# A second line for the attention heads, and stick-breaking heads that ask for their values last

## The chip, the core and the metric

One Trainium2 chip, one core. The metric is device time in microseconds (us) of one execution of the kernel. A core has a matrix engine (TensorE, written PE in the profile, with its weight loads as PEld), a vector engine (VectorE, DVE), a scalar engine (ScalarE, ACT), GpSimd (POOL) and a queue of loads and stores (SyncE, SP). In the built program each engine has its own list of instructions; an instruction that waits holds up those that stand behind it in that list.

## What is computed

One layer of a hybrid encoder over 256 tokens of width 2048, in float32:

```python
h = rms_norm(x)                                   # x: (256, 2048)
proj = h @ w_in                                   # q, k, v of 8 "fox" heads, gates, q, k, v of 8 "sb" heads
# fox head: softmax(q_t.k_s/sqrt(128) + c[t] - c[s]), s <= t, times v; q and k are normed per head
# sb head:  z = q_t.k_s/sqrt(128); weights exp(log_sigmoid(z) + sum of log(1 - sigmoid) between s and t), s < t, times v
x = x + concat(rms_norm(out_fox), rms_norm(out_sb)) @ w_out
x = x + conv_ffn(rms_norm(x))                     # up-projection, width-3 causal convolution, SiLU gate, down-projection
```

## The kernel before

**Precision.** TensorE gets every float32 operand as a pair: `hi`, the value rounded to a shorter format (a copy on ScalarE, line 201), and `lo = raw - hi` (a subtraction on VectorE, line 202). A product is then three products: hi by hi, lo by hi, hi by lo.

**Steps.** All projections are cut into steps of 1 MB of weights. A step loads `w_raw` (line 194, three buffers in this part), makes `w_hi` and `w_lo` (two buffers each), and runs 16 matmuls on `w_hi` and then 8 (or 16 half-wide ones) on `w_lo`, all 512 columns or less: `token_major` (line 223; weights stream past the tokens) for values, fox queries and keys and `w_out`, `feature_major` (lines 250 and 257) for the stick-breaking queries and keys. Load and splits are written with a high priority, so they run about two steps ahead of their matmuls.

**What lies between the steps.** The attention itself is written as Python generators, each cut into stages by `yield`. They stand in one queue, `waiting`. After every step of a projection, `step()` (line 181) advances the first two generators of the queue (`WINDOW = 2`) by one stage each. So the order in which instructions are issued to the framework is: one step's matmuls, one stage each of two generators, the next step, and so on. The framework's scheduler then orders each engine's instructions by priority and by when it thinks their inputs are there. From the feed-forward part on, the order is written by hand and the scheduler changes nothing.

**The generators.**

- `fox_rows` (line 306): evicts a projection, norms q or k per head (square, sum, reciprocal root, product; lines 317 to 322), waits, transposes each 128-token tile on TensorE (line 298) and stores it in parts (lines 302, 304).
- `gates`: the forget gates and their running sum.
- `fox_head` (line 591): waits until the generators that stood in the queue when it was made are gone (`first`). Stage 1: scores (lines 598, 513), bias, mask and softmax (lines 605 to 619). After two more turns, stage 2: three transposes of the probabilities (line 624) and their split (627 to 629). Stage 3: the product with the values (581, 582) and `attended` (347 to 356), which stores the head's output and adds up its squares.
- `sb_head` (line 701). Stage 1: scores `ps_z` (lines 513, 708), the soft-plus on ScalarE (712 to 714), then `sp` (718, 719) and its split `sps` (721, 722). Stage 2: two products of `sps` with a triangular matrix, hi then lo, which make the suffix sums inside `ps_z` (727, 728), one exponential (730) and the split of the weights (732 to 736). Stage 3: as for a fox head. The tile `sp` has one buffer, `sps` and the score tiles (PSUM) have two, and so has the PSUM pool that holds transposes and head outputs.
- `next_rows`: transposes of the new x for the feed-forward part.

**The order of the projections:** in an opening written by hand the fox queries of heads 0 to 3, then fox values (with the gates' columns), fox keys of heads 0 to 3, fox queries and keys of heads 4 to 7, then for each half of the stick-breaking heads its queries, keys and values, then `w_out` in two groups of eight heads. A fox head joins the queue when its keys' generator has joined. A stick-breaking head joins once its half's values stand: it takes the tile `v` as an argument.

Of the kernel before, what the change touches and what calls it, by code (L numbers as in the profile page):

```python
# [36 lines left out]
WINDOW = 2  # L37
# [8 lines left out]
def hybrid_layer(  # L46
# [129 lines left out]
        return R  # L176


    waiting = deque()

    def step():
        for g in list(waiting)[:WINDOW]:
            if next(g, g) is g:
                waiting.remove(g)

    def finish():
        while waiting:
            step()


# [87 lines left out]
    with ExitStack() as actx:  # L278
# [9 lines left out]
        def project(c0, cols):  # L288
            return token_major(lambda k: hT[:, k], wi, 0, KT, c0, cols)
# [46 lines left out]
        def attended(po, h, g, group):  # L336

            if len(done) == NH:

                two = late.tile([P, 2, 2, S], F32R, name="oT89", tag="two_heads")  # L340
                oT.extend([two[:, 0], two[:, 1]])
                oT.extend(late.tile([P, 2, S], F32R, name=f"oT{i}") for i in range(NH + 2, 2 * NH - 4))
                oT.extend(hT[:, KT - 4 + i] for i in range(4))
            done.append(group * NH + h)
            assert done[-1] == len(done) - 1
            o = oT[group * NH + h]
            act.activation(o[:, 0, :], po, AF.Identity, scale=g[:, h : h + 1])
            dve.scalar_tensor_tensor(
                o[:, 1, :], po, g[:, h : h + 1], f32(o[:, 0, :]), op0=ALU.mult, op1=ALU.subtract
            )  # L350
            if h == 0:
                act.activation(ssq[group], po, AF.Square)
            else:
                sq = tmp.tile([P, S], F32, name="osq", tag="t1", bufs=3)
                act.activation(sq, po, AF.Square)
                dve.tensor_tensor(ssq[group], ssq[group], sq, op=ALU.add)
# [218 lines left out]
        def weighted(v, hs, w):  # L575


            wp, w1 = w
            po = psb.tile([P, S], F32, name="ps_o", tag="t")
            for i, (j, k) in enumerate(((0, 0), (0, 1), (1, 0))):  # L580
                nc.tensor.matmul(po, v[j][:, hs], wp[:, k], start=i == 0, stop=False)
            nc.tensor.matmul(po[:, P:], v[2][:, hs], w1, start=False, stop=True)
            return po
# [7 lines left out]
        def fox_head(h, qT, kT, first):  # L591
            while any(g in waiting for g in first):
                yield
            yield
            ps = pss.tile([P, 3, P], F32, name="ps_s", tag="s")
            s0, s1 = ps[:, 0, :], ps[:, 1:3, :].rearrange("p a b -> p (a b)")
            j = h % 4
            nc.tensor.matmul(s0, qT[0][0][:, j, :], kT[0][0][:, j, :], start=True, stop=False)
            of_parts(s1, [t[:, j, :] for t in qT[1][1:]], [t[:, j, :] for t in kT[2]], False, True)
            scored.append(h)  # L600
            pr = tmp.tile([P, 3, P], F32, name="pr", tag="pr")
            p0, p1 = pr[:, 0, :], pr[:, 1:3, :].rearrange("p a b -> p (a b)")

            for o, s, t in ((p0, s0, 0), (p1, s1, 1)):
                dve.scalar_tensor_tensor(
                    o, minus_c[h // 4][:, h % 4, : (t + 1) * P], c_of[:, t, h : h + 1], s, op0=ALU.add, op1=ALU.add
                )
            diagonal = pr[:, 0::2, :]
            dve.tensor_tensor(diagonal, diagonal, mask2, op=ALU.add)
            nm = small.tile([P, NT], F32, name="nm", tag="nm")  # L610
            dve.tensor_reduce(nm[:, 0:1], p0, axis=AX.X, op=ALU.max, negate=True)
            dve.tensor_reduce(nm[:, 1:2], p1, axis=AX.X, op=ALU.max, negate=True)
            l = small.tile([P, NT], F32, name="l", tag="l")
            act.activation(p0, p0, AF.Exp, bias=nm[:, 0:1], accum_out=l[:, 0:1])
            act.activation(p1, p1, AF.Exp, bias=nm[:, 1:2], accum_out=l[:, 1:2])
            rl = small.tile([P, NT], F32, name="rl", tag="rl")
            dve.reciprocal(rl, l)
            dve.tensor_scalar(p0, p0, rl[:, 0:1], None, op0=ALU.mult)
            dve.tensor_scalar(p1, p1, rl[:, 1:2], None, op0=ALU.mult)
            yield  # L620
            yield
            pt = pss.tile([P, 3, P], F32, name="ps_p", tag="s")
            for i in range(3):
                nc.tensor.transpose(pt[:, i, :], pr[:, i, :], ident)
            pT, pT1 = weights_tiles("pT")
            pt0 = pt[:, 0:2, :].rearrange("p a b -> p (a b)")
            act.copy(pT[:, 0], pt0)
            act.copy(pT1, pt[:, 2, :])
            dve.tensor_tensor(pT[:, 1], pt0, f32(pT[:, 0]), op=ALU.subtract)
            yield  # L630
            attended(weighted(vA, slice(h * HD, (h + 1) * HD), (pT, pT1)), h, g_fox, 0)

        for half in range(2):
            if half:
                qT = fox_queries(1)
                waiting.append(fox_rows(project(512, 512), qT, gq))
                step()
            else:
                qT = qT0
            kT = fox_keys(half)  # L640
            waiting.append(fox_rows(project(WF + 512 * half, 512), kT, g_k))
            step()
            first = list(waiting)
            for h in range(4 * half, 4 * half + 4):
                waiting.append(fox_head(h, qT, kT, first))


        B0 = 3 * WF + NH
# [52 lines left out]
        def sb_head(h, qT, kT, v):  # L701
            (q1, *q), (k1, *k) = qT[h % 4], kT[h % 4]
            ps = pss.tile([P, 3, P], F32, name="ps_z", tag="s")
            z0, z1 = ps[:, 0:2, :].rearrange("p a b -> p (a b)"), ps[:, 2, :]
            zz = ps.rearrange("p a b -> p (a b)")
            mm = nc.tensor.matmul
            of_parts(z0, k, q, True, False)
            mm(z1, k1, q1, start=False, stop=True)
            scored.append(NH + h)

            e = tmp.tile([P, 3 * P], F32, name="e", tag="pr")
            act.activation(e, zz, AF.Abs)
            act.activation(e, e, AF.Exp, scale=-1.0)
            act.activation(e, e, AF.Ln, bias=1.0)
            sp = tmp.tile([P, 3, P], F32, name="sp", tag="sp", bufs=1)
            diagonal = sp[:, 0::2, :]
            sp = sp.rearrange("p a b -> p (a b)")
            dve.scalar_tensor_tensor(sp, zz, 0.0, e, op0=ALU.max, op1=ALU.add)
            dve.tensor_tensor(diagonal, diagonal, limit2, op=ALU.min)
            sps = tmp.tile([P, 2, 3 * P], F32R, name="sps", tag="sps")  # L720
            act.copy(sps[:, 0, :], sp)
            dve.tensor_tensor(sps[:, 1, :], sp, f32(sps[:, 0, :]), op=ALU.subtract)
            yield

            for i in range(2):
                s = sps[:, i, :]
                mm(zz, ntri[:, :P], s, start=False, stop=False, skip_group_check=True)
                mm(ps[:, 1, :], ntri[:, P:], s[:, 2 * P :], start=False, stop=i == 1, skip_group_check=True)
            e = tmp.tile([P, 3, P], F32, name="e", tag="pr")
            act.activation(e, ps, AF.Exp)  # L730
            w, w1 = weights_tiles("w")
            dve.tensor_tensor(e[:, 0, :], e[:, 0, :], limit, op=ALU.min)
            e0 = e[:, 0:2, :].rearrange("p a b -> p (a b)")
            act.copy(w[:, 0], e0)
            dve.tensor_tensor(w1, e[:, 2, :], limit, op=ALU.min)
            dve.tensor_tensor(w[:, 1], e0, f32(w[:, 0]), op=ALU.subtract)
            yield
            attended(weighted(v, slice((h % 4) * HD, (h % 4 + 1) * HD), (w, w1)), h, g_sb, 1)

        for half in range(2):  # L740
            qT = sb_queries(half)
            kT = sb_keys(half)
            acc = project(B0 + 2 * WF + 512 * half, 512)

            assert scored[:4] == [0, 1, 2, 3]
            v = [
                at.tile([P, 512], dt, name=f"{name}{half}", tag=tag, bufs=1)
                for name, dt, tag in (("vB", F32R, "vB"), ("vBlo", F32R, "minus_c0"), ("vBt1", F32, "vBt1"))
            ]
            values(v, acc)  # L750
            for h in range(4 * half, 4 * half + 4):
                waiting.append(sb_head(h, qT, kT, v))


        ss2 = const.tile([P, NT, 4], F32, name="ss2")
# [398 lines left out]
```

## Time and profile before

| | |
|---|---|
| median of 3 runs | 1107.34 us (1106.92 to 1107.37) |
| span of the profiled execution (first to last instruction) | 1104.9 us |
| median less span (what lies around the span) | 2.4 us |
| TensorE busy in the span | 1099.6 us |
| VectorE, ScalarE, GpSimd busy | 870.4, 706.3, 44.0 us |
| attention part, from the first fox scores to the last head's product | about 123 to 345 us |

No device time of its own is listed for the profiled execution; its span stands 2.4 us below the median of the runs, and that distance is carried along unchanged in what follows.

Rows of groups read: line, engine, operation, output <- inputs, shapes, count | busy us, mean ns of one | idle time of the engine just before, and who ended it. Rows of a timeline read: start in us, length in us, engine, line, operation, names, shape, count, and in brackets the idle time before it. Matmuls overlap each other, so the length of a row of matmuls is longer than its share of TensorE's time: that share is the distance from its start to the start of the next row.

### The profile page before, as it was taken

The page shows a single profiled execution, that of the slowest core. Times are in us where ns is not written, and L with a number is a line of the kernel's source. Part 1 is how long each engine was busy: PE and PEld are TensorE (multiplying, and loading weights), DVE is VectorE, ACT ScalarE, POOL GpSimd, SP SyncE. Part 2 cuts the span into 40 slices and gives each one's busy share as a digit, 9 for nine tenths or more (in the row PEclk, how much of TensorE's full clock was granted, in tenths as well). Part 3 has the DMA queues.
Part 4 walks back from the last instruction along what each step waited for, and adds up shares of the span by engine and source line. Part 5 has one row for each costly group of instructions (what it writes and reads, how often), then busy time and mean ns, then how long its engine had stood idle before and what let it go on. Part 6 is the DMA issues. An engine that isn't in the chain of part 4 may idle for free. (4 is left out here: it accounts for less than half of the span.)

```text
span 1104.9 us, 14836 instructions
## 1 busy us (share of the span) xinstructions
PE 1099.6 (100%) x5880; PEld 953.9 (86%) x5880; DVE 870.4 (79%) x941; ACT 706.3 (64%) x879; POOL 44.0 (4%) x44
## 2 busy tenths in 40 slices
PE   9999999999999999999999999999999999999998
PEld 7998888888888888888888888888888888888887
DVE  6755767667676677679889888889798889889896
ACT  6543555457674567667767776667676677677753
POOL 0000000000000000000000010100000010100010
PEclk9999999999999999999999999999999999999999
DMA  8776555555644396557989597986979689987985
GB/s 285 195 232 229 187 164 180 173 170 169 242 156 158 114 304 200 190 189 195 301 210 323 191 229 264 260 269 178 315 210 306 213 218 281 245 264 196 324 212 168
DMA packets 179407, 246.09 MB, mean 223 GB/s; under 512 B 4432, under 2 KB 118890, under 8 KB 179082
## 3 DMA queue, kind: packets, MB, share of 16 engines
q1 hardware_dynamic: 162458, 209.87, 58.3%
q0 software_dynamic: 16560, 34.75, 16.7%
q8 instruction: 46, 0.75, 0.3%
q10 hardware_dynamic: 320, 0.53, 0.1%
q14 instruction: 23, 0.19, 0.0%
HBM read 243.02 MB, written 2.11 MB: 222 GB/s over the span
## 5 line engine op out<-in xcount | busy, mean ns | idle before, releaser
L202 DVE TENSOR_TENSOR w_lo<-w_raw,w_hi 128x2048 fp32r<-128x2048 f32 (+1 forms) x196 | 439.7, 2246 | 155.0 <-ACT w_hi L201 153.2
L201 ACT CAST w_hi<-w_raw 128x2048 fp32r<-128x2048 f32 (+1 forms) x196 | 367.1, 1875 | 247.4 <-PE pu L250 68.9
L250 PE MATMUL pu<-hT,w_hi 128*128 128x512 f32 x1664 | 396.7, 390 | 0.0
L250 PEld LDWEIGHTS pu<-hT,w_hi 128*128 128x128 f32 x1664 | 309.4, 188 | 62.6
L257 PEld LDWEIGHTS pu<-hT,w_lo 128*128 128x128 f32 x1664 | 213.7, 191 | 8.3
L257 PE MATMUL pu<-hT,w_lo 128*128 128x256 f32 x1664 | 216.4, 283 | 0.0
L223 PE MATMUL acc<-w_hi,hT 128*128 128x512 f32 (+1 forms) x576 | 124.9, 369 | 0.0
L223 PEld LDWEIGHTS acc<-w_hi,hT 128*128 128x128 f32 x576 | 101.2, 188 | 14.2
L201 ACT CAST w_hi<-w_sum 128x2048 fp32r<-128x2048 f32 x30 | 57.2, 1908 | 42.0 <-PE pu L250 35.8
L202 DVE TENSOR_TENSOR w_lo<-w_sum,w_hi 128x2048 fp32r<-128x2048 f32 x30 | 68.7, 2290 | 19.0 <-ACT w_hi L201 19.0
L851 ACT ACTIVATE tap<-up,ccol 128x256 f32<-128x256 f32 x176 | 74.6, 495 | 0.0
L223 PE MATMUL acc<-w_lo,hT 128*128 128x512 f32 (+1 forms) x288 | 64.6, 366 | 0.0
L223 PEld LDWEIGHTS acc<-w_lo,hT 128*128 128x128 f32 x288 | 51.6, 188 | 7.5
L956 POOL DMA_DIRECT2D w_sum<-in_w_down_dram x20 | 25.7, 1284 | 742.8 <-DVE w_lo L202 732.1
L223 PE MATMUL acc<-w_hi,oT 128*128 128x512 f32 x192 | 46.5, 394 | 0.0
L223 PEld LDWEIGHTS acc<-w_hi,oT 128*128 128x128 f32 x192 | 35.4, 188 | 7.2
L223 PE MATMUL bank_a<-w_hi,s 128*128 128x512 f32 x160 | 40.1, 392 | 0.2 <-DVE x L933 0.2
L223 PE MATMUL bank_a<-w_hi,g 128*128 128x512 f32 x160 | 40.0, 392 | 0.0
L223 PE MATMUL bank_b<-w_hi,s 128*128 128x512 f32 x160 | 40.0, 392 | 0.0
L223 PEld LDWEIGHTS bank_a<-w_hi,s 128*128 128x128 f32 x160 | 28.8, 189 | 5.8 <-issue 0.6
L223 PEld LDWEIGHTS bank_a<-w_hi,g 128*128 128x128 f32 x160 | 28.9, 189 | 5.3
L223 PEld LDWEIGHTS bank_b<-w_hi,s 128*128 128x128 f32 x160 | 28.9, 189 | 5.2
(215 smaller groups left out, 1077.5 us busy)
## 6 DMA issues: line engine op xcount, KB each, us to landing
w_raw<-in_w_up_dram SPq DMA_DIRECT2D x88, 1024.0 KB, 7.9
w_raw<-in_w_down_dram SPq DMA_DIRECT2D x44, 1024.0 KB, 6.6
w_raw<-in_w_in_dram SPq DMA_DIRECT2D x36, 1024.0 KB, 5.3
w_sum<-in_w_down_dram POOLq DMA_DIRECT2D x20, 1024.0 KB, 10.3
w_raw<-in_w_out_dram SPq DMA_DIRECT2D x16, 1024.0 KB, 5.1
w_raw<-in_w_down_dram POOLq DMA_DIRECT2D x10, 1024.0 KB, 14.7
w_raw<-in_w_in_dram SPq DMA_DIRECT2D x12, 688.0 KB, 4.3
w_raw<-in_w_in_dram SPq DMA_DIRECT2D x6, 512.0 KB, 7.1
```

The source lines that it names most:

```text
L201: act.copy(hi[:, :n], raw[:, :n])
L202: dve.tensor_tensor(lo[:, :n], raw[:, :n], f32(hi[:, :n]), op=ALU.subtract)
L223: nc.tensor.matmul(o, lhs(i, l, t), r[:, i, :], start=starts and j == 0, stop=stops and j == 3 * n - 1, skip_group_check=more,)
L250: nc.tensor.matmul(acc[:, j, :], hi[:, i, j * P : (j + 1) * P], hT[:, k].rearrange("p a b -> p (a b)"), start=k == 0, stop=False,)
L257: nc.tensor.matmul(acc[:, j, S:], lo[:, i, j * P : (j + 1) * P], hT[:, k, 0, :], start=False, stop=k == KT - 1,)
L851: act.activation(taps[w][:, j, :], u[:, j, w : w + S], AF.Copy, scale=ccol[:, w, f : f + 1])
L956: nc.gpsimd.dma_start(mem[into][:, : nk * 512].rearrange("p (a b) -> p a b", a=nk), src, accum_op=ALU.add)
```

## The change

There are two queues now: `waiting` for norms, gates and transposes, `heads` for all attention heads. `step()` advances the first two of each. A fox head's `first` then lists generators of `waiting` alone. A stick-breaking head joins `heads` as soon as its keys are projected, ahead of its half's value projection, with an empty list in the place of the values; its last stage turns idle until the list is filled.

```diff
-    waiting = deque()
+    waiting, heads = deque(), deque()
 
     def step():
-        for g in list(waiting)[:WINDOW]:
-            if next(g, g) is g:
-                waiting.remove(g)
+        for q in (waiting, heads):
+            for g in list(q)[:WINDOW]:
+                if next(g, g) is g:
+                    q.remove(g)
 
     def finish():
-        while waiting:
+        while waiting or heads:
             step()
...
             for h in range(4 * half, 4 * half + 4):
-                waiting.append(fox_head(h, qT, kT, first))
+                heads.append(fox_head(h, qT, kT, first))
...
             yield
+            while not v:
+                yield
             attended(weighted(v, slice((h % 4) * HD, (h % 4 + 1) * HD), (w, w1)), h, g_sb, 1)
 
         for half in range(2):
             qT = sb_queries(half)
             kT = sb_keys(half)
+            v = []
+            earlier = list(heads)
+            for h in range(4 * half, 4 * half + 4):
+                heads.append(sb_head(h, qT, kT, v))
             acc = project(B0 + 2 * WF + 512 * half, 512)
 
-            assert scored[:4] == [0, 1, 2, 3]
-            v = [
+            assert not half or not any(g in heads for g in earlier)
+            v.extend(
                 at.tile([P, 512], dt, name=f"{name}{half}", tag=tag, bufs=1)
                 for name, dt, tag in (("vB", F32R, "vB"), ("vBlo", F32R, "minus_c0"), ("vBt1", F32, "vBt1"))
-            ]
+            )
             values(v, acc)
-            for h in range(4 * half, 4 * half + 4):
-                waiting.append(sb_head(h, qT, kT, v))
```

The built order of instructions shows what becomes of it. No matmul, copy or transfer is added or dropped, and from the last quarter of `w_out` on every engine's order is as before; so are the orders of SP and POOL throughout. In between, two heads now go through their stages side by side (the scores of both, then the transposes of both, then the products of both), where before one head followed the other by a step. The last stick-breaking product stands three steps earlier.

## The prediction

> **What bounds the kernel now.** I read the page first: busy time, then the span in slices.
>
> ```profile
> PE 1099.6 (100%) x5880; PEld 953.9 (86%) x5880; DVE 870.4 (79%) x941; ACT 706.3 (64%) x879; POOL 44.0 (4%) x44
> PE   9999999999999999999999999999999999999998
> PEclk9999999999999999999999999999999999999999
> ```
>
> TensorE is busy in every slice, at full granted clock. Busy does not mean at its peak, so the second view is who kept TensorE waiting.
>
> ```profile
> PE idle L372 <- DVE zeros L362: 1.1, 1, 1.1
> PE acc L419 <- DVE w_hi L400: 0.6, 1, 0.6
> PE bank_a L223 <- DVE x L933: 0.2, 1, 0.2
> PE ps_h L298 <- DVE rs_u L117: 0.2, 1, 0.2
> ```
>
> Only the last of the four lies in the attention part, the only part that the change reorders. The third view is TensorE's timeline there, read by distances between starts. A step without attention work:
>
> ```profile
> 95.19 3.79 PE L223 MATMUL acc<-w_hi,hT 128*128 128x512 f32 x16
> 98.81 1.98 PE L223 MATMUL acc<-w_lo,hT 128*128 128x512 f32 x8
> 100.63 3.79 PE L223 MATMUL acc<-w_hi,hT 128*128 128x512 f32 x16
> ```
>
> It takes 3.62 + 1.82 = 5.44 us. From 95 to 426 us I found every step at this pace (feature-major steps at 5.56), plus the head work between them, save one place:
>
> ```profile
> 194.67 0.75 PE L257 MATMUL pu<-hT,w_lo 128*128 128x256 f32 x5
> 195.61 0.63 PE L298 MATMUL ps_h<-cs,raw 128*128 128x128 f32 x4 [0.19 <-DVE rs_u L117]
> 195.99 1.56 PE L257 MATMUL pu<-hT,w_lo 128*128 128x256 f32 x11
> 197.39 0.60 PE L298 MATMUL ps_h<-cs,raw 128*128 128x128 f32 x4
> ```
>
> ```profile
> 194.77 0.69 DVE L322 TENSOR_TENSOR raw<-raw,r 128x512 f32<-128x512 f32 x1
> ```
>
> The scheduler cut a `w_lo` pass to set in transposes when it thought `raw` ready. Five matmuls at (197.39 - 195.99 - 0.10, a start-up explained in (b))/11 = 0.12 need 0.6 and took 0.94: a stall of **0.34 us**. `raw` ended at 195.46, TensorE started 0.15 later. So the attention part holds 0.34 us that a better order could win, and a worse order can only add. The opening's and the tail's waits lie outside the change.
>
> **The change, part by part.**
>
> (a) *Work.* The built order holds the same instructions: nothing is added on any engine; SP and POOL keep their orders, so no load moves in its queue. Everything that comes is position.
>
> (b) *Interruptions.* A piece of head work between steps costs more than itself: the 512-wide pass behind it starts slowly. The suffix products alone, a head's product, and a product followed by suffix products:
>
> ```profile
> 290.69 0.33 PE L727 MATMUL ps_z<-sps,masksR 128*128 128x384 f32 x1
> ...
> 291.20 0.34 PE L513 MATMUL ps_z<-qB,low 128*128 128x256 f32 x1
> ...
> 297.33 0.41 PE L581 MATMUL ps_o<-w,vB 128*128 128x256 f32 x2
> ...
> 297.83 0.42 PE L727 MATMUL ps_z<-sps,masksR 128*128 128x384 f32 x1
> ...
> 298.43 3.88 PE L223 MATMUL acc<-w_hi,oT 128*128 128x512 f32 x16
> 302.15 1.98 PE L223 MATMUL acc<-w_lo,oT 128*128 128x512 f32 x8
> ```
>
> Suffix products: 0.51. Product: 0.50; suffix products behind it: 0.60, so 0.09 more. The pass behind: 3.72, so 0.10 more than 3.62. I counted the interruptions between the first fox scores and the second `w_out` group: 36 in the old order, 37 in the new. Pairing heads merges pieces, but the old order merged too (one head's product with the next head's scores), and the new one cuts pieces apart. That is +0.10. Inside the merged pieces the short-then-long joints that cost about 0.07 rise from some 11 to some 15, within the counting's error: +0.1 here, bounds -0.3 to +0.6. **Term: +0.2.**
> The Trainium skill, "TensorE: Matmul & The Clock Gate", section "Step-by-step: what each phase is for", says that TensorE pulls the next weight load ahead of running matmuls; by that an interruption would cost nothing beyond its own work, and the sum below would be 0.2 lower. The 0.10 in the rows above speaks against it here.
>
> (c) *The stall that goes.* Those transposes now stand directly behind a step or behind the other transposes. **Term: -0.34.**
>
> (d) *New waits on TensorE.* Two heads' elementwise work now falls into the time that one had, between the scores and the piece that needs their result. The order says where TensorE then stands; I added up both sides at each such place from these rows:
>
> ```profile
> L202 DVE TENSOR_TENSOR w_lo<-w_raw,w_hi 128x2048 fp32r<-128x2048 f32 x40 | 91.6, 2291 | 62.6 <-ACT w_hi L201 61.4 <-PE pu L257 1.2
> L722 DVE TENSOR_TENSOR sps<-sp,sps 128x384 fp32r<-128x384 f32 x8 | 4.5, 559 | 3.4 <-ACT sps L721 3.4
> L612 DVE TENSOR_REDUCE nm<-pr 128x1 f32<-128x256 f32 x8 | 3.3, 410 | 0.0
> L609 DVE TENSOR_TENSOR pr<-pr,masksR 128x256 f32<-128x256 f32 x8 | 3.4, 422 | 0.1
> L611 DVE TENSOR_REDUCE nm<-pr 128x1 f32<-128x128 f32 x8 | 2.3, 285 | 0.2
> L618 DVE TENSOR_SCALAR pr<-pr,rl 128x128 f32<-128x128 f32 x8 | 2.2, 281 | 0.0
> L115 DVE TENSOR_TENSOR rs_u<-rs_a,rs_y 128x4 f32<-128x4 f32 x6 | 0.8, 155 | 0.0
> ```
>
> ```profile
> 302.35 1.91 ACT L201 CAST w_hi<-w_raw 128x2048 fp32r<-128x2048 f32 x1 [1.29 <-PE acc L223]
> ...
> 308.88 0.51 ACT L721 CAST sps<-sp 128x384 fp32r<-128x384 f32 x1 [0.83 <-DVE sp L719]
> 309.30 1.91 ACT L201 CAST w_hi<-w_raw 128x2048 fp32r<-128x2048 f32 x1
> ```
>
> ```profile
> 103.17 1.28 DVE L317 TENSOR_TENSOR sq<-raw 128x512 f32<-128x512 f32 x2
> 104.37 1.27 DVE L319 TENSOR_REDUCE ss<-sq 128x4 f32<-128x512 f32 x2
> ```
>
> ```profile
> 208.76 0.38 PE L598 MATMUL ps_s<-kA,qA 128*128 128x128 f32 x2
> ...
> 209.34 3.81 PE L223 MATMUL acc<-w_hi,hT 128*128 128x512 f32 x16
> 212.99 1.98 PE L223 MATMUL acc<-w_lo,hT 128*128 128x512 f32 x8
> ```
>
> A `w_hi` cast starts 0.20 after its pass (302.15, 302.35). An independent instruction starts 0.08 to 0.09 before its predecessor's recorded end (104.37 against 104.45; 309.30 against 309.39); call the rest its slot. For a late moving operand I take 0.06 from the elementwise end to TensorE, an estimate between the 0.03 that VectorE needs after ScalarE (304.29, the next `w_lo`, after 302.35 + 1.91) and the 0.15 above.
>
> ```profile
> 304.29 2.29 DVE L202 TENSOR_TENSOR w_lo<-w_raw,w_hi 128x2048 fp32r<-128x2048 f32 x1 [2.74 <-ACT w_hi L201]
> ```
>
> *Stick-breaking heads 4 and 5*, in the values' projection; zero is the end of both heads' `ps_z`. On ScalarE the second head's `sps` cast stands behind a `w_hi` cast: 3.72 (pass) + 0.20 + 1.91 - 0.09 + 0.51 = 6.25. TensorE comes to it at 3.72 + 1.82 + 0.51 (first head) = 6.05, so it waits until 6.31: 0.26. Eight matmuls later it wants the second head's `sps` low part; that stands on VectorE behind the `w_lo` that began at 3.72 + 0.20 + 1.91 + 0.03 = 5.86: 5.86 + 2.29 - 0.08 + 0.56 = 8.63, 8.69 at TensorE, which is there at 6.31 + 0.31 + 0.10 + 8 x 0.226 = 8.53: 0.16. Sum 0.42. What waits behind these on TensorE is the step itself. The other three pairs by the same addition: 0.06 (heads 0, 1: cut two matmuls later), 0.25 (2, 3), 0.08 (6, 7).
>
> *Fox heads 0 and 1*; zero is the end of both scores (0.58 each; the pass behind them takes 3.65). VectorE is bound by its second `w_lo`: 3.65 + 0.20 + 1.91 + 0.03 = 5.79, next slot at 8.00. Then, before the first head's first product with `rl`: eight tiny norm steps (0.6 in all), `nm` twice 0.20 and twice 0.33, the second head's mask 0.34, two `raw` products 1.20 (0.69 each, by the row of 194.77), a reciprocal as short as a norm step 0.07: 3.27, so it starts at 11.27 and ends at 11.55; with 0.15, TensorE gets it at 11.70. TensorE is there after two steps and four transposes (3.65 + 1.82 + 5.44 + 0.38 = 11.29; the transposes by 195.61 to 195.99): 0.41. The later cuts of this pair and those of heads 2 and 3 come out between 0 and 0.1 early; heads 4 to 7 have no `raw` work beside them, and their transposes are ready 0.6 or more ahead. **Term: 0.41 + 0.42 + 0.06 + 0.25 + 0.08 = +1.22.**
>
> (e) *Weights.*
>
> ```profile
> L713 ACT ACTIVATE e<-e 128x384 f32<-128x384 f32 x8 | 4.2, 527 | 0.3
> L714 ACT ACTIVATE e<-e 128x384 f32<-128x384 f32 x8 | 4.2, 526 | 0.3
> L712 ACT ACTIVATE e<-ps_z 128x384 f32<-128x384 f32 x8 | 3.9, 493 | 1.1 <-PE ps_z L708 0.8
> ```
>
> A second head's first stage in the same step gives ScalarE 0.53 + 0.53 + 0.49 + 0.51 = 2.1 us more to do. A `w_hi` cast is ready 0.20 + 1.91 after its pass, and needed only after its `w_lo` pass and one more step, 1.82 + 5.44 = 7.26: the cover is 5.1 us, so I cost this at nothing. If the cover went, each step would be late by what exceeds it.
>
> (f) *Heads that end three steps earlier, values asked for last.* TensorE did not wait for either before, so nothing is won. For heads 0 to 3 the built order places the scores behind the values' projection anyway.
>
> **Sum:** +0.2 - 0.34 + 1.22 = +1.1 us on the span of 1104.9, so 1106.0; with the 2.4 around it, and against the median of 1107.34, **1108.4 us**.
>
> **The rivals.** *Every cut waits as the old one did.* The new order sets head pieces into a pass, or behind a result timed to the moment, at about 15 places. The single place of this kind in the old order stalled 0.34. At that rate: 15 x 0.34 - 0.34 + 0.2 = +5.0, **1112.3**, slower. It decides from a mean of (2.2 + 0.34 - 0.2)/15 = 0.16 a place; my sum has 0.08. For it: one measured place. Against it: the additions, several of which end early.
>
> *Pairing wins.* If the joints cost nothing and each of the 16 pairings spared one start-up of 0.10, the change would be worth -1.6 - 0.34: **1105.4**; with a little more, faster. Against it: the count of 36 and 37. The Trainium skill, "Perfetto Trace Analysis", section "Identifying the Most-Contended Engine", wants TensorE's headroom judged by the busy share of weight loads, not of matmuls. The page of the profile has 86% there, which by that rule leaves room; the steps' even 5.44 us, with and without heads beside them, show no use of it by order.
>
> *Late weights.* If the bursts of (e) outran their cover by 1 us at four places, +4 us, **1112.4**. Against it: 2.1 against 5.1.
>
> *It does nothing:* the pairing moves stalls of equal size, **1107.3**. This falls within my forecast.
>
> **How the numbers follow.** About 0.2% (2.2 us) is what a measurement of this kernel can tell from no change. Forecast, within 0.2%: 0.74. Every cut waits: 0.19, late weights: 0.04, together slower 0.23. Pairing wins by over 0.2%: 0.03. The low end of the range is no new stall at all with the lower bound of (b), -0.34 - 0.3: 1106.7. The high end takes half the way to the first rival, with 0.22 a place: 15 x 0.22 - 0.34 + 0.6 = 3.6: 1110.9. Below and above lie about 0.05 and 0.12.
>
> **What would show it.** Right: TensorE's waits after list `ps_p` on VectorE's `pr` and `ps_z` on `sps`, each a few tenths; the step pace unchanged; the sum of those waits near 1.2. Wrong: gaps in `acc` or `pu` passes on `w_hi` (late weights), waits at the heads' products, or a feed-forward part of another length.

## The result and the profile after

| | before | after |
|---|---|---|
| median, 21 runs each | 1106.88 us (1106.56 to 1108.87) | 1108.51 us (1108.14 to 1109.19) |
| span of the profiled execution | 1104.9 us | 1106.7 us |
| first fox scores to the first `bank_a` product of the feed-forward part | 381.13 us | 382.89 us |

The ratio is 1.0015, with a 95% interval of 1.0009 to 1.0021: 1.6 us slower, within the 0.2% forecast as no change. The time is 0.1 us from the one forecast, but that is luck, as told further down. The third row of the table is the measure for everything below. It is read from the starts of two rows of TensorE's timeline, and leaves out the opening, whose length differs by up to 0.45 us between profiled executions. Before and after, these two rows are:

```profile
123.38 0.38 PE L598 MATMUL ps_s<-kA,qA 128*128 128x128 f32 x2
...
504.51 2.00 PE L223 MATMUL bank_a<-w_hi,g 128*128 128x512 f32 x8
```

```profile
123.36 0.38 PE L599 MATMUL ps_s<-kA,qA 128*128 128x128 f32 x2
...
506.25 2.00 PE L224 MATMUL bank_a<-w_hi,g 128*128 128x512 f32 x8
```

So the whole loss, 1.76 us, lies in this stretch. The page of the changed kernel has TensorE 2.0 us longer busy with the same 5880 matmuls (1101.6 against 1099.6), at the same clock, but tells neither place nor cause:

```profile
PE 1101.6 (100%) x5880; PEld 953.2 (86%) x5880; DVE 870.3 (79%) x941; ACT 705.0 (64%) x879; POOL 44.0 (4%) x44
...
PEclk9999999999999999999999999999999999999999
```

Nor does the list of TensorE's waits. The old wait of `ps_h` has gone from it, and nothing has come in its place:

```profile
PE idle L373 <- DVE zeros L363: 1.1, 1, 1.1
PE acc L420 <- DVE w_hi L401: 0.4, 1, 0.4
PE bank_a L224 <- DVE x L938: 0.3, 1, 0.3
```

The same list for TensorE's weight loads (PEld) does tell. Its columns are: who waited for what; us in total, times, longest.

```profile
PEld ps_z L728 <- DVE sps L723: 1.5, 4, 0.4
...
PEld ps_z L728 <- ACT sps L722: 0.8, 3, 0.4
...
PEld ps_o L582 <- DVE low L305: 0.5, 2, 0.3
PEld ps_p L625 <- DVE pr L619: 0.3, 1, 0.3
```

Seven suffix products wait for `sps`, one transpose waits for `pr`, and two products of fox heads with the values wait until VectorE has emptied a transposed key or query tile (`low` from `ps_h`), which takes one of the two PSUM buffers that they share. In the kernel before no `ps_z`, no `ps_p` and no `ps_o` stands in this list. These idle times overlap with running matmuls, so they aren't yet the price. The price is in the starts. Stick-breaking heads 4 and 5 after, TensorE and then its weight loads:

```profile
290.31 0.33 PE L728 MATMUL ps_z<-sps,masksR 128*128 128x384 f32 x1
290.49 0.22 PE L729 MATMUL ps_z<-sps,masksR 128*128 128x128 f32 x1
290.55 0.39 PE L728 MATMUL ps_z<-sps,masksR 128*128 128x384 f32 x1
290.77 0.22 PE L729 MATMUL ps_z<-sps,masksR 128*128 128x128 f32 x1
291.07 0.45 PE L728 MATMUL ps_z<-sps,masksR 128*128 128x384 f32 x1
291.36 0.22 PE L729 MATMUL ps_z<-sps,masksR 128*128 128x128 f32 x1
291.42 2.05 PE L224 MATMUL acc<-w_hi,hT 128*128 128x512 f32 x8
293.46 0.44 PE L728 MATMUL ps_z<-sps,masksR 128*128 128x384 f32 x1
293.74 0.22 PE L729 MATMUL ps_z<-sps,masksR 128*128 128x128 f32 x1
```

```profile
290.49 0.19 PEld L728 LDWEIGHTS ps_z<-sps,masksR 128*128 128x128 f32 x1
...
291.07 0.19 PEld L728 LDWEIGHTS ps_z<-sps,masksR 128*128 128x128 f32 x1 [0.28 <-ACT sps L722]
...
293.46 0.19 PEld L728 LDWEIGHTS ps_z<-sps,masksR 128*128 128x128 f32 x1 [0.41 <-DVE sps L723]
```

The distance from 290.77 to 291.07 is 0.30 where 0.06 is usual (290.49 to 290.55): the second head's first suffix product waits 0.24. Eight 512-wide matmuls from 291.42 take 2.04. At 0.227 each they need 1.82, the first has a slow start of 0.07 (in the run e6 below, six of them behind a ready product take 1.43 in place of 1.36, 287.26 to 288.69), and the rest, 0.15, is the wait for the second head's low part. And the two late products themselves take 0.29 and 0.28 to the next start, where the first head's took 0.18 and 0.22. Their weight loads start with them, at 291.07 and 293.46; the load at 290.49 started 0.06 ahead of its product. ScalarE and VectorE show who was in the way:

```profile
288.70 1.91 ACT L202 CAST w_hi<-w_raw 128x2048 fp32r<-128x2048 f32 x1 [0.27 <-PE acc L224]
290.52 0.50 ACT L722 CAST sps<-sp 128x384 fp32r<-128x384 f32 x1
```

```profile
290.65 2.29 DVE L203 TENSOR_TENSOR w_lo<-w_raw,w_hi 128x2048 fp32r<-128x2048 f32 x1 [0.50 <-ACT w_hi L202]
292.86 0.55 DVE L723 TENSOR_TENSOR sps<-sp,sps 128x384 fp32r<-128x384 f32 x1
```

The `sps` cast behind `w_hi` ends at 291.02, its low part behind `w_lo` at 293.41, and TensorE starts 0.05 after each.

### The profile page after: what moved, and what is told of

Same layout as the page of the kernel before. It is cut to its first block, busy times and chain, and to the rows that moved or that the text cites. A ratio compares the mean times of both kernels' runs of the same rounds, so it can differ in the third digit from the quotient of the medians.

```text
span 1106.7 us, 14832 instructions
## 1 busy us (share of the span) xinstructions
PE 1101.6 (100%) x5880; PEld 953.2 (86%) x5880; DVE 870.3 (79%) x941; ACT 705.0 (64%) x879; POOL 44.0 (4%) x44
```

## The experiments

The theory after this reading: a head's second result is late because two heads' elementwise work falls into one head's time, and each late product costs its wait and more. The rivals: pieces cut into passes cost by themselves; joints of paired pieces cost; it is the early joining and not the pairing. "Stretch" is the third row of the table above, read in the same way for each kernel. The recorded expectations number the stick-breaking heads 8 to 15; in the text here they are 0 to 7. The runs came in two groups, beside runs of the kernel before with medians of 1106.84 (the first four) and 1107.18 us (the last four).

| kernel | median, us | ratio to before, 95% | span | stretch |
|---|---|---|---|---|
| e1_split_only | 1108.47 | 1.0016 (1.0007 to 1.0025) | 1107.2 | 382.87 |
| e2_slack | 1106.34 | 0.9995 (0.9986 to 1.0004) | 1104.6 | 380.69 |
| e3_fox_slack | 1108.38 | 1.0015 (1.0006 to 1.0024) | 1106.4 | 382.49 |
| e4_two_sp | 1108.34 | 1.0013 (1.0005 to 1.0022) | 1106.6 | 382.70 |
| e5_casts_first | 1109.13 | 1.0017 (1.0008 to 1.0026) | 1107.3 | 382.99 |
| e6_cuts_alone | 1106.92 | 0.9999 (0.9990 to 1.0008) | 1105.0 | 380.94 |
| e7_uncut | 1113.92 | 1.0064 (1.0050 to 1.0078) | 1112.0 | 387.85 |
| e8_mirror | 1106.58 | 0.9995 (0.9986 to 1.0004) | 1105.0 | 380.59 |

**e1: the split of the queue alone.**

```diff
-            for h in range(4 * half, 4 * half + 4):
-                heads.append(sb_head(h, qT, kT, v))
             acc = project(B0 + 2 * WF + 512 * half, 512)
...
             values(v, acc)
+            for h in range(4 * half, 4 * half + 4):
+                heads.append(sb_head(h, qT, kT, v))
```

> The queue is split, but a stick-breaking head joins after its values again, as in the kernel before. Theory (the loss of 1.8 us of span is made where two heads go in step: their second results come late, and their pieces are cut into passes): the fox part and the first two stick-breaking pairs are placed as in the changed kernel, only the last two pairs move, so the span stays at 1106.7, give or take 0.3. Rival (the heads that join early and ask for their values last bring the loss): the span falls back to between 1104.9 and 1105.4.

The stretch is 382.87 against 382.89 of the changed kernel: the split with its pairing makes the whole loss by itself, and joining early adds nothing to it. The span is 0.5 longer because the first scores start 0.42 later, ahead of anything that differs.

**e2 and e3: one turn more ahead of the piece that needs the result.**

```diff
             dve.tensor_scalar(p1, p1, rl[:, 1:2], None, op0=ALU.mult)
             yield
             yield
+            if h < 4:
+                yield
...
             dve.tensor_tensor(sps[:, 1, :], sp, f32(sps[:, 0, :]), op=ALU.subtract)
             yield
+            yield
```

(e3 has the first of the two additions only.)

> The changed kernel with one turn more between the scores and the piece that needs their result (all stick-breaking heads, fox heads 0 to 3). Heads still go in pairs; by the built order no piece is cut into a pass, and 34 pieces stand between steps where there were 43. Theory (late results 1.2 us, cuts some 1.0): adding up the places' distances between starts without waits and cuts, -0.38 at the fox heads and -1.82 at the stick-breaking heads, so a span of 1104.5, 0.4 under the kernel before. Rival 1 (only the late results cost, and the joints of paired pieces stay): -1.2, 1105.5. Rival 2 (pieces between steps cost about 0.1 each, so nine fewer are worth 0.9 more): 1103.6. Rival 3 (the waits only move): 1106.2 or more.

> One turn more for fox heads 0 to 3 alone. Theory: the wait before their first transposes (0.21) and the start-ups of the cut pieces of heads 0 and 1 go, those of heads 2 and 3 come out even: -0.38, a span of 1106.3. Rival (the three cuts into passes cost 0.3 each): -0.9, 1105.8.

e2: -2.20 against the changed kernel, as the theory had it to the second digit. e3: -0.40, close to the theory's -0.38; at its median of 1108.38 this is too small to be seen in the times. Its list of weight-load waits has lost the waits of `ps_p` and of `ps_o`, and kept those of `ps_z`. In e2's list none of the three stands any more, and the four suffix products of a pair stand whole, 1.09 long (285.42 to 286.51):

```profile
285.42 0.33 PE L731 MATMUL ps_z<-sps,masksR 128*128 128x384 f32 x1
285.59 0.22 PE L732 MATMUL ps_z<-sps,masksR 128*128 128x128 f32 x1
...
285.93 0.39 PE L731 MATMUL ps_z<-sps,masksR 128*128 128x384 f32 x1
286.16 0.22 PE L732 MATMUL ps_z<-sps,masksR 128*128 128x128 f32 x1
...
286.51 3.88 PE L224 MATMUL acc<-w_hi,hT 128*128 128x512 f32 x16
```

Rival 2 falls with it: nine pieces fewer between steps brought nothing beyond the places themselves. e2's stretch is 0.44 shorter than that of the kernel before, of which 0.35 is the old stall of `ps_h`. Its times can't be told from the kernel before.

**e4: a second buffer for `sp`.**

```diff
-            sp = tmp.tile([P, 3, P], F32, name="sp", tag="sp", bufs=1)
+            sp = tmp.tile([P, 3, P], F32, name="sp", tag="sp", bufs=2)
```

> The changed kernel with two buffers for the tile sp instead of one, so that VectorE need not wait with the second head's soft-plus until the first head's split is done. Theory (the second head's cast to sps misses its turn ahead of the w_hi cast because its sp waits for that single buffer): the waits of 0.13 and 0.24 before the second head's suffix products go, heads 8 and 9 come out uncut (-0.46) and heads 14 and 15 lose one of two cuts (-0.15): together -1.0 (-0.6 to -1.2), a span of 1105.7. Rival (the cast is late because ScalarE is full, whatever the buffers): no change, 1106.7.

A miss: -0.19. The second head's `sp` does come earlier, but not its cast. In heads 4 and 5 VectorE finished `sp` at 288.81, and ScalarE was free at 287.89 (287.37 + 0.52), yet its order has `w_hi` first:

```profile
287.37 0.52 ACT L722 CAST sps<-sp 128x384 fp32r<-128x384 f32 x1 [0.31 <-DVE sp L720]
288.43 1.91 ACT L202 CAST w_hi<-w_raw 128x2048 fp32r<-128x2048 f32 x1 [0.55 <-PE acc L224]
290.25 0.50 ACT L722 CAST sps<-sp 128x384 fp32r<-128x384 f32 x1
```

```profile
288.39 0.42 DVE L720 TENSOR_TENSOR sp<-sp,masksR 128x256 f32<-128x256 f32 x1
```

Heads 0 and 1 came out uncut and without a wait; heads 6 and 7, in place of one of their two cuts, got a wait of 0.25 at the second head's first product. So what holds the cast back is the order on ScalarE, not the buffer.

**e5: the casts ahead of the splits.** The cast of the second head's `sps` is made to stand ahead of the third `w_hi` cast issued after it, and the low part ahead of that `w_lo`.

```diff
+        with behind[0]():
             act.copy(hi[:, :n], raw[:, :n])
+        with behind[1]():
             dve.tensor_tensor(lo[:, :n], raw[:, :n], f32(hi[:, :n]), op=ALU.subtract)
...
+            if h % 2:
+                second.append([3, lambda: tc.issue_after(cast.ins), lambda: tc.issue_after(low_part.ins)])
```

> The changed kernel, with the second head's cast to sps queued on ScalarE ahead of the w_hi cast that stood before it, and its low part on VectorE ahead of the w_lo. By the built order the suffix products of heads 10 to 13 come out whole, and the second head's product with the values is cut into a pass at three places instead. Theory (the second head's sps is late because it stands behind w_hi and w_lo): the waits of 0.13 + 0.10 and 0.24 + 0.15 in these two pairs go, with their cuts -1.0; the three cut products give back 0.1 to 0.5; a span of 1105.7 to 1106.3. Rival (the sps are late by their own chain): the waits at the whole suffix products of these pairs grow to the depth of the old cuts, 1.8 to 2.5 each, a span of 1109 or more.

Half a miss. Where the order could be turned, the long waits are gone: in heads 4 and 5 the suffix products stand whole, 1.08 from 291.38 to 292.46, as in e2, and in heads 2 and 3 they stand whole with a wait of 0.13 for the low part (265.73 to 265.92 in place of 0.06). In heads 0 and 1 the waits grew from 0.18 to 0.5. And the stretch is 0.10 longer than the changed kernel's. The list of weight-load waits says where it went:

```profile
PEld ps_o L592 <- ACT w L747: 0.9, 3, 0.4
...
PEld ps_z L740 <- DVE sps L733: 0.5, 2, 0.3
PEld ps_z L740 <- ACT sps L732: 0.4, 1, 0.4
PEld ps_o L592 <- DVE w L749: 0.3, 1, 0.3
```

The waits for `sps` fell from 2.3 to 0.9, and four new ones, 1.2 together, stand at the products with the values, whose `w` is now late. Much of the lateness moved a stage on. Of the kernels run, only the one with a turn more (e2) takes it away.

**e6: cuts without lateness.** On e2, the low half of each suffix product goes into the next pass.

```diff
         for j, (i, l, r) in enumerate(order):
+            if j in (2, 5) and mid:
+                mid.pop(0)()
...
+            suffix(0)
+            mid.append(rest)
```

(`rest` does the low half and what follows it; the feature-major passes get the same two lines.)

> The kernel of e2_slack, in which no piece is cut and no result late (span 1104.6), with the low half of all eight stick-breaking suffix products set by hand into the middle of the following pass, a head at a time; their operands have been ready for a step by then. The built order has eight such cuts, and one cut product with the values besides. Theory C (a cut costs by itself, 0.14 each, as the rest of the loss in the changed kernel shared out over its six suffix cuts): +1.2, a span of 1105.8. Theory W (what a cut costs is that the product is late: it waits, and its weight load of 0.11 is not drawn ahead while it waits; a cut with ready operands is nearly free): 0 to +0.3, a span of 1104.6 to 1104.9.

Theory W: the stretch is 0.25 longer than e2's with nine more cuts, 0.03 each. The first cut product of heads 4 and 5, and its weight load:

```profile
287.03 0.33 PE L739 MATMUL ps_z<-sps,masksR 128*128 128x384 f32 x1
287.20 0.22 PE L740 MATMUL ps_z<-sps,masksR 128*128 128x128 f32 x1
287.26 1.59 PE L228 MATMUL acc<-w_hi,hT 128*128 128x512 f32 x6
```

```profile
286.80 0.19 PEld L739 LDWEIGHTS ps_z<-sps,masksR 128*128 128x128 f32 x1
```

The load starts 0.23 ahead of its product, and the product takes 0.17 to the next start. In the changed kernel the same product, in the same kind of place, took 0.28 with its load starting beside it: 0.11 that lateness costs beyond the wait.

**e7: the late products left whole.**

```diff
+        with behind_heads():
             for j, (i, l, r) in enumerate(order):
...
+            if h % 2:
+                ends[:] = [last]
```

(`behind_heads` queues the pass on TensorE behind the second head's last suffix product.)

> The changed kernel, with the next pass queued on TensorE behind the second head's suffix product: in the last three pairs the suffix products come out whole, so TensorE must wait for the late halves. Theory (the cuts stand where the late operands are just about ready, so they hide nearly all of the delay): the waits grow by the depth of the old cuts, 11, 8 and 9 matmuls of 0.227, together 6.3, less what the cuts cost, 0.5: a span of 1110 to 1112.5. Rival (the operands were there long before, and cutting only cost): a span of 1106.3 or less.

The span of 1112.0 is inside the theory's range, though partly by luck. Without their cuts the second pair waits 2.6 us and the third 1.3, so there the cuts do hide most of the delay. But the last pair came out whole without any wait, for a reason not looked into; the waits are 3.9 together in place of 6.3. The difference was made up by something unforeseen behind the second pair's wait, which cost 1.6 and is told in the last section.

**e8: the short products side by side.**

```diff
-            of_parts(z0, k, q, True, False)
-            mm(z1, k1, q1, start=False, stop=True)
+            if h % 2:
+                mm(z1, k1, q1, start=True, stop=False)
+            of_parts(z0, k, q, h % 2 == 0, h % 2 == 1)
+            if h % 2 == 0:
+                mm(z1, k1, q1, start=False, stop=True)
```

(The fox scores are turned in the same way.)

> The kernel of e2_slack (span 1104.6), in which the first head of a pair takes its 128-wide score product last and the second head takes it first, so that the two short products of a pair stand side by side, and of the long products only one per pair stands behind a short one. Theory J (a long product behind a short one costs 0.085, as the rows of joints read): eight joints fewer, -0.7, a span of 1103.9. Theory L (whatever stands behind a short product waits for its own weight load, a short one as well as a long one, so that the order doesn't matter): no change, 1104.6, give or take 0.15.

Theory L: 380.59 against 380.69. (The span of 1105.0 is longer than e2's because the first scores start 0.39 later.) The rows show the price moving with the short product: at heads 0 and 1 the pass behind the piece, which now ends on a long product, takes 3.62 (249.15 to 252.77; e2: 3.72), and the first head's two short products, now ahead of the second head's, take 0.22 (248.35 to 248.57; e2: 0.14). So a joint has no price of its own: whatever stands behind a short product starts late. That it is the weight load that it waits for is theory L's reason, and no run tests it by itself.

## Why the prediction was right, and where it was not

The sum was +1.1 us on the span, measured were +1.8. That the time forecast, 1108.4 us, was met within 0.1 is luck: the sum was 0.7 too small, and the 2.4 us carried from the span to the median were 0.6 too many. They were the median of some executions less the span of another. In each listed execution of either kernel the time is 1.7 to 1.8 us above its own span (after: 1108.51 and 1106.7). The parts of the sum:

(a) *Work*: right; the instruction counts on the page are the same. (f) *Heads that end earlier, values asked last*: right, by e1. (e) *Late weights*: right; steps without heads keep their pace in the changed kernel (3.62 + 1.82):

```profile
130.00 3.79 PE L224 MATMUL acc<-w_hi,hT 128*128 128x512 f32 x16
133.62 1.99 PE L224 MATMUL acc<-w_lo,hT 128*128 128x512 f32 x8
135.44 0.60 PE L299 MATMUL ps_h<-cs,raw 128*128 128x128 f32 x4
136.09 0.33 PE L625 MATMUL ps_p<-cs,pr 128*128 128x128 f32 x1
```

(c) *The stall that goes*: right, 0.35 (forecast 0.34); e2 and the changed kernel have none there.

(d) *New waits*: right in place and cause, but for two products that it lacked, told below. The sum is right too, but in part by luck: single places are off by up to a factor of three, and cancel. Read as above, the waits are:

| place | forecast | measured |
|---|---|---|
| fox heads 0, 1 | 0.41 | 0.21 |
| stick-breaking 0, 1 | 0.06 | 0.12 + 0.06 |
| 2, 3 | 0.25 | 0.13 + 0.10 |
| 4, 5 | 0.26 + 0.16 | 0.24 + 0.15 |
| 6, 7 | 0.08 | 0.15 |
| sum | 1.22 | 1.16 |

The fox wait is in the rows above: from 135.44 to 136.09 the transposes took 0.65, and four transposes with another behind them need 0.44 (heads 2 and 3, 161.85 to 162.29). On VectorE, the product that they wait for:

```profile
135.76 0.28 DVE L619 TENSOR_SCALAR pr<-pr,rl 128x128 f32<-128x128 f32 x1
```

The addition held (it started 11.24 after the scores' end at 124.52, forecast 11.27), but TensorE followed its end by 0.05, where the prediction had taken the 0.15 of the old stall, and came there 0.06 later itself, the four transposes taking 0.44 in place of 0.38. The 0.06 taken elsewhere was right.

What failed is the price of a late product in (d): it was charged its wait alone. A late product also loads its weights in the open. At the eight late suffix products (one of them, in heads 6 and 7, late by too little for the list of waits) the distance to the next start is 0.24 to 0.29, against 0.17 or 0.23 for the same product when ready, by its place in the piece (e2: 285.42 to 285.59, 285.93 to 286.16). The differences, 0.05 to 0.11 each, add up to 0.72. The term is missing from the sum; with it the sum is 0.2 - 0.34 + 1.22 + 0.72 = 1.8. The two products of fox heads that wait for a PSUM buffer were missing as well: a sign of being wrong that the prediction itself had named, waits at the heads' products. They hardly wait (about 0.03 each by the starts, an estimate), but pay the same price:

```profile
145.67 0.49 PE L582 MATMUL ps_o<-pT,vA 128*128 128x256 f32 x2
146.00 0.28 PE L582 MATMUL ps_o<-pT,vA_low 128*128 128x256 f32 x1
...
172.78 0.45 PE L582 MATMUL ps_o<-pT,vA 128*128 128x256 f32 x2
173.06 0.28 PE L582 MATMUL ps_o<-pT,vA_low 128*128 128x256 f32 x1
```

They take 0.33 and 0.28 to the next row where ready ones in this place take 0.24 (199.84 to 200.08), so 0.13 together.

(b) *Interruptions*: after waits (1.16), loads (0.72 and 0.13) and the stall that went (0.35), 0.1 of the 1.76 remains, by subtraction, for all changes of position, against a term of 0.2. So the size held within its bounds; but its reading did not. The 0.10 behind a head piece is not a price of interrupting: e2 stands with 34 interruptions where the changed kernel has 43 (over a longer range than the prediction's 36 and 37; over that one e2 has 28), and beyond waits and loads it gained no more than 0.2 by that, and e6 sets nine more for 0.03 each. It belongs to the short product that stands last in the piece, and moving it about neither saves nor costs (e8). The rule of the Trainium skill, "TensorE: Matmul & The Clock Gate", section "Step-by-step: what each phase is for", that weight loads are pulled ahead of running matmuls, was set aside there on too little: e6 agrees with it for operands that are ready (the load 0.23 ahead), and the changed kernel shows its limit, a load that waits for the product's late operand (`sps`) and starts beside it, though `sps` is not what it loads. Whether the chip or the built program puts the wait on the load, no run shows.

"What would show it" named the right pairs, `ps_p` on `pr` and `ps_z` on `sps`, in the wrong list: the matmuls' list shows none of them, since ends are modelled; the weight loads' list shows all but the shortest.

The rivals: *Every cut waits as the old one did* would have needed 5 us; the waits measured, 1.16 over its 15 or so places, are 0.08 each, as in the sum, and e7 shows what two pairs wait without cuts. *Pairing wins* is refuted by e2, which pairs without any lateness and gains 0.09 beyond the old stall. *Late weights*: no step shows any. *It does nothing*: the distances say otherwise, by 1.76.

## What to carry to other kernels

Before two chains of work are set side by side, add up on each engine what then stands ahead of the second chain's results, a weight split included; if the matrix engine arrives first, give the chain a turn more, since moving single instructions ahead, in e5, made the next stage late. Cutting small products into a long pass is nearly free when their operands are ready (0.03 us each here); when they are late, count the wait and an open weight load, here 0.05 to 0.11 us. Look for such waits in the list of weight loads and in the distances between starts, not in the matmuls' own waits.

## What the runs showed of the hardware

In e7 TensorE waited 2.67 us between two starts (265.48 to 268.15). The stretches of that time, with the granted clock in the column behind the five engines:

```profile
265.50:268.10 2.60, 0.20 (x2) 0.00 (x0) 2.60 (x4) 0.53 (x2) 0.00 (x0) 1.00 0.98 388
268.10:269.50 1.40, 1.35 (x6) 1.16 (x7) 1.40 (x5) 1.16 (x4) 0.00 (x0) 0.82 0.99 339
269.50:270.50 1.00, 1.00 (x4) 0.81 (x3) 0.99 (x4) 0.66 (x3) 0.00 (x0) 0.50 1.04 403
...
272.50:274.00 1.50, 1.50 (x9) 1.24 (x8) 0.00 (x0) 0.00 (x0) 0.00 (x0) 1.00 0.00 0
```

About a microsecond after the wait the clock fell to half, and stayed there for some 3 us. The pass of 16 matmuls behind the wait took 5.32 instead of 3.70 us (268.49 to 273.81; the same pass in e2, 261.04 to 264.74), so a wait of 2.6 cost 1.6 more. The wait of 1.3 in the third pair was not followed by a lower clock. The Trainium skill, "TensorE: Matmul & The Clock Gate", section "HAM oscillation — how this bites in real kernels", asks for no idle gap of more than about 3.4 us; here one of 2.6 between starts (2.45 idle in the profile) was enough, seen at one place.
